# A two-block sequence model on one core: selection pinned on VectorE with new tick prices, and the MLP's two input parts in one matmul

## The chip, the core and the metric

The kernel runs on one core of one Trainium2 chip. Time is device time in microseconds (us) from a run of the whole program; the number that counts is the median of the runs. TensorE (PE) multiplies, VectorE (DVE) and ScalarE (ACT) do the elementwise work, GpSimd (POOL) issues the gathers, SyncE (SP) issues the weight loads.

## The reference

256 tokens of width 2048 pass through two blocks. Only the parts that the change touches are spelled out.

```python
# first block, last part
f = jnp.square(jax.nn.relu(rms_norm(h, norm_mlp_pre[i]) @ mlp_w1[i])) @ mlp_w2[i]   # 2048 -> 8192 -> 2048
h = h + rms_norm(f, norm_mlp_post[i])
...
# second block, last part: 16384 experts, 8 heads, 16 experts for each head and token
q = (x @ wq).reshape(B, S, PEER_HEADS, 2, half)
s = jnp.einsum('bshpd,pkd->bshpk', q, subkeys)          # 2 x 128 scores per head
s1, i1 = lax.top_k(s[..., 0, :], PEER_TOPK)
s2, i2 = lax.top_k(s[..., 1, :], PEER_TOPK)
cand_s = s1[..., :, None] + s2[..., None, :]
top_s, pos = lax.top_k(cand_s, PEER_TOPK)
gate = jax.nn.softmax(top_s, axis=-1)
ue = jnp.take(u_tab, it, axis=0)
ve = jnp.take(v_tab, it, axis=0)
act = jax.nn.gelu(jnp.einsum('td,ted->te', xt, ue), approximate=False)
out = jnp.einsum('te,ted->td', gt * act, ve)
```

## The kernel before, in words

Everything is float32. A weight is split into two parts that TensorE takes at its fast rate, `whi` (the rounded value) and `wlo` (the rest), and so is each input: a tile `x[k]` of 128 x 2 x 256 holds the high part of 256 tokens and, behind it without a gap, the low part. A product needs three terms: `whi` by both parts and `wlo` by the high part.

**Blocks.** The unit of the program is a block of 128 x 2048 weights: `chunk` loads it in two halves (SP), writes `whi` on ScalarE and `wlo` on VectorE, and 16 steps of k multiply it into one PSUM tile. Four half-block buffers of each kind hold two blocks, so VectorE can be at most about one block ahead of the one being multiplied. There are 528 blocks. `chunk` is recorded with high priority, so the scheduler may place its work ahead of what was recorded earlier.

- `mm3` does a step of k as three matmuls of 256 columns.
- `mm2` does it as two: `whi` by both parts at once, into the two halves of a PSUM bank, then `wlo` by the high part into the first half. Somebody has to add the halves later. Before the change only the expert stage uses it, with 224 tokens: 448 and 224 columns.

**MLP.** `mlp_groups` runs four groups, each of 16 blocks of `w_m1` (the square of the ReLU goes to tiles `Bx`) and 16 blocks of `w_m2` (added into `acc`): 128 blocks in all.

**Expert stage.** `route` computes the queries (16 blocks of `w_q`) and selects per head; `route_tail` selects among the pairs and builds the tables of experts. One selection of 16 out of a list (`top16`) is five VectorE instructions; there are 32 lists of 128 and 16 of 80. 32 tokens are then done sparsely: `sparse` gathers 256 rows (128 of u, 128 of v; POOL), and VectorE multiplies each. The other 224 tokens are done densely with all the experts: blocks `w_u` (`peer_u`: ScalarE copies one PSUM half to `pu`, VectorE adds the other, ScalarE applies Gelu) and blocks `w_v` (added into `hT`), in 8 groups of 16 and 16.

**What sets the order.** The selection, the tables and the sparse rows are Python generators. `tick(n)` is called after a block and lets the current generator go on for n units; a `yield w` costs w units, and `yield GAP` stops it till the next tick. The constants are the units per block: `TR` in `route`, `TD` in the tail and the table stage, `TSP` for the sparse rows (u blocks, v blocks). `flush()` in the last expert group runs at once what is left. Within this recorded order the scheduler still moves instructions; `keep_in_program_order` ties one behind the last instruction recorded on its engine.

Of the kernel before, what the change touches and what calls it, by code (L numbers as in the profile page):

```python
# [14 lines left out]
ALU = mybir.AluOpType  # L15
# [19 lines left out]
NF = 2  # L35
# [5 lines left out]
NG = 5  # L41
S0 = 6
UPRE = (3, 5, 8, 8)
TR = 1.5
GU = 4
TD = (1.35, 4.95)
NT = 16
PJ = 4
T8 = 2
# [2 lines left out]
NQ = 128 // SP  # L52
QW = 2048 // NQ
NR = 5
TSP = (1.15, 1.6)
WX = 2
NPRE = 64
PG = NPRE // 8
# [190 lines left out]
class Kern:  # L249
# [161 lines left out]
    def mm2(self, w, x, n, p=None, last=True):  # L411


        nc = self.nc
        first = p is None
        if first:
            p = self.psm.tile([128, 512], F32, name="mm")[:, :2 * n].rearrange("p (c t) -> p c t", c=2)
        m = len(w)
        for k in range(m):
            nc.tensor.matmul(p, w[k][0], x[k][:, :, :n], start=(first and k == 0), stop=False)  # L420
            nc.tensor.matmul(p[:, 0], w[k][1], x[k][:, 0, :n], start=False, stop=(last and k == m - 1))  # L421
        return p

    def blocks(self, srcs, x, first=2):

# [539 lines left out]
    def mlp_groups(self, rm):  # L965
        nc = self.nc
        acc = self.accp.tile([128, 16, 256], F32, name="acc")
        ssq = {}
        for g in range(4):
            hid = []  # L970
            for hb, p in enumerate(self.blocks([self.I["w_m1"][16 * g + i] for i in range(16)], self.xs, 1 if g else NF)):
                if (g, hb) == (0, S0):
                    self.push(self.s5_setup())
                self.tick(TS)
                t = self.T([128, 256], "mr")
                nc.vector.scalar_tensor_tensor(t, p, 0.0, rm(), op0=ALU.max, op1=ALU.mult)
                s = self.T([128, 256], "msq")
                nc.scalar.activation(s, t, AF.Square)
                hid.append(self.split("B", hb, s))
            for nb in range(16):  # L980
                if (g, nb) == (3, 8):
                    self.warm_sqrt()
                p = self.mmps()
                self.mm3(p, self.chunk(self.I["w_m2"][16 * g + nb]), hid)
                if g == 0:
                    nc.vector.tensor_copy(acc[:, nb], p)
                else:
                    nc.vector.tensor_tensor(acc[:, nb], acc[:, nb], p, op=ALU.add)
                if g == 3:
                    self.ssq_add(ssq, acc[:, nb])  # L990
        return acc, ssq
# [471 lines left out]

    def top16(self, v, i, src, s2, w):
        V = self.nc.vector
        V.max(out=v[:, 0:8], in_=src)
        V.max_index(out=i[:, 0:8], in_max=v[:, 0:8], in_values=src)
        yield 2 * w
        V.match_replace(out=s2, in_to_replace=v[:, 0:8], in_values=src, imm_value=-3e38)
        V.max(out=v[:, 8:16], in_=s2)  # L1470
        V.max_index(out=i[:, 8:16], in_max=v[:, 8:16], in_values=s2)
        yield 3 * w
# [63 lines left out]
    def route_head(self, h, sc):  # L1536
        for tb in range(2):
            for half in range(2):
                s2 = self.T([128, 128], "rs2")
                yield from self.top16(self.rv[half][:, tb, h], self.ri[half][:, tb, h], sc[tb][:, half], s2, 0.2)  # L1540

    def route_tail(self):
        nc = self.nc
        V = nc.vector
# [12 lines left out]
        for tb in range(2):  # L1557
            for h in range(8):
                s2 = self.T([128, 80], "rs3")
                yield from self.top16(tv[:, tb, h], ti[:, tb, h], cand[:, tb, h], s2, 0.15)  # L1560
        ex = B([128, 2, 8, 16], "rex")
        V.tensor_tensor(ex, tv, tv[:, :, :, 0:1].to_broadcast([128, 2, 8, 16]), op=ALU.subtract)
        for tb in range(2):
# [322 lines left out]
```

## Time and profile before

| | |
|---|---|
| median of 3 runs | 3260.41 us (3260.27 to 3267.97) |
| profiled execution, its own time | 3260.36 us |
| its span, first to last instruction | 3258.6 us |
| PE / PEld / DVE / ACT / POOL busy | 98 / 93 / 75 / 52 / 19 % |

The profile is of one execution that agrees with the median, so differences can be taken from the span. A PE that is busy 98% need not be at full speed: the number of matmuls that start in a stretch of time tells whether it is.

### The profile page before, as it was taken

To read this page: it belongs to the slowest core of one execution; us is meant where nothing else is said; L and a number is where in the kernel's file an instruction comes from. 1 tells how busy PE (TensorE), PEld (TensorE's weight loads), DVE (VectorE), ACT (ScalarE), POOL (GpSimd) and SP (SyncE) were. 2 spreads that over 40 slices of the span, in tenths; PEclk is the share of its full clock that TensorE was granted. 3 is DMA by queue.
4 is the path that set the end of the run, shared out by engine and by line. 5 is a ranking of instruction groups with operands and counts; after the bars stand their busy time and mean duration, and the time that the engine had idled before them with its cause. 6 is when DMAs were issued, how large, how long until landed. Compare 5 with 4: busy or idle time off the path is not lost.

```text
span 3258.6 us, 59733 instructions
## 1 busy us (share of the span) xinstructions
PE 3178.6 (98%) x23207; PEld 3021.6 (93%) x23207; DVE 2429.8 (75%) x4226; ACT 1695.5 (52%) x2556; POOL 618.4 (19%) x669
## 2 busy tenths in 40 slices
PE   8999989999999999999999989999999999999988
PEld 7888989999999999888899989899999999999987
DVE  5577786575756567898968875775888888888876
ACT  5567555363545445454545445565454454454443
POOL 2001130000000011100003001002334344444432
PEclk9999999999999999999999989999999999999999
DMA  8343546575666555544445457678989989989974
GB/s 272 133 128 118 170 138 209 187 230 193 215 201 197 191 162 182 191 156 160 145 148 175 158 189 229 218 253 280 318 285 326 314 286 313 316 288 315 316 243 150
DMA packets 217645, 708.29 MB, mean 217 GB/s; under 512 B 26944, under 2 KB 53200, under 8 KB 215568
## 3 DMA queue, kind: packets, MB, share of 16 engines
q1 hardware_dynamic: 174208, 579.94, 53.2%
q0 software_dynamic: 31728, 100.98, 9.3%
q10 hardware_dynamic: 11424, 23.55, 2.0%
q8 instruction: 182, 2.98, 0.4%
q14 instruction: 103, 0.84, 0.1%
HBM read 668.16 MB, written 35.15 MB: 216 GB/s over the span
## 4 chain that ended last, share of the span: by engine, by line
PE 44%; DVE 8%; ACT 2%; issue 1%; DMA 0%; DVEq 0%; ACTq 0%; SPq 0%
PE mm L420 21%; PE mm L421 10%; DVE wlo L397 3%; PE mm L407 3%; PE mm L408 3%; PE mm L409 3%; PE sm L1657 1%; PE oT L1220 1%; ACT whi L396 1%; DVE spa L1700 1%; DVE Bx L1782 1%; DVE pa L1774 1%; ACT pa L1670 1%; ACT Bx L1779 1%; DVE pu L1668 1%
## 5 line engine op out<-in xcount | busy, mean ns | idle before, releaser
L396 ACT CAST whi<-raw 128x1024 fp32r<-128x1024 f32 x1056 | 1098.3, 1048 | 1131.3 <-PE mm L408 577.7
L397 DVE TENSOR_TENSOR wlo<-raw,whi 128x1024 fp32r<-128x1024 f32 x1056 | 1292.9, 1231 | 505.2 <-ACT whi L396 499.9
L420 PE MATMUL mm<-Ax,whi 128*128 128x448 f32 x2048 | 654.8, 379 | 0.6 <-ACT whi L396 0.6
L420 PE MATMUL mm<-Bx,whi 128*128 128x448 f32 x2048 | 645.5, 376 | 4.0 <-DVE Bx L1782 3.8
L407 PE MATMUL mm<-Bx,whi 128*128 128x256 f32 x2192 | 625.1, 285 | 0.0
L408 PE MATMUL mm<-Bx,whi 128*128 128x256 f32 x2192 | 621.6, 284 | 0.0
L407 PE MATMUL mm<-Ax,whi 128*128 128x256 f32 x2128 | 607.8, 288 | 13.6 <-ACT Ax L449 5.3
L409 PE MATMUL mm<-Bx,wlo 128*128 128x256 f32 x2192 | 620.9, 283 | 0.0
L408 PE MATMUL mm<-Ax,whi 128*128 128x256 f32 x2128 | 607.4, 286 | 2.0 <-DVE Ax L450 1.6
L409 PE MATMUL mm<-Ax,wlo 128*128 128x256 f32 x2128 | 605.2, 285 | 1.5 <-DVE wlo L397 1.5
L421 PE MATMUL mm<-Ax,wlo 128*128 128x224 f32 x2048 | 544.0, 266 | 14.2 <-DVE wlo L397 14.2
L421 PE MATMUL mm<-Bx,wlo 128*128 128x224 f32 x2048 | 539.9, 264 | 0.0
L407 PEld LDWEIGHTS mm<-Ax,whi 128*128 128x128 f32 x2128 | 409.4, 193 | 24.7 <-issue 6.7
L407 PEld LDWEIGHTS mm<-Bx,whi 128*128 128x128 f32 x2192 | 420.2, 192 | 9.5 <-issue 9.3
L408 PEld LDWEIGHTS mm<-Bx,whi 128*128 128x128 f32 x2192 | 420.5, 192 | 2.3 <-issue 2.2
L409 PEld LDWEIGHTS mm<-Bx,wlo 128*128 128x128 f32 x2192 | 420.3, 192 | 1.1 <-issue 1.0
L420 PEld LDWEIGHTS mm<-Bx,whi 128*128 128x128 f32 x2048 | 384.8, 188 | 35.7 <-DVE Bx L1782 5.9
L420 PEld LDWEIGHTS mm<-Ax,whi 128*128 128x128 f32 x2048 | 388.7, 190 | 31.3 <-ACT whi L396 0.8
L408 PEld LDWEIGHTS mm<-Ax,whi 128*128 128x128 f32 x2128 | 410.8, 193 | 6.5 <-DVE Ax L450 2.5
L409 PEld LDWEIGHTS mm<-Ax,wlo 128*128 128x128 f32 x2128 | 410.8, 193 | 4.8 <-DVE wlo L397 2.0
L421 PEld LDWEIGHTS mm<-Ax,wlo 128*128 128x128 f32 x2048 | 394.8, 193 | 17.5 <-DVE wlo L397 17.4
L421 PEld LDWEIGHTS mm<-Bx,wlo 128*128 128x128 f32 x2048 | 391.3, 191 | 0.2 <-DVE wlo L397 0.2
(465 smaller groups left out, 3256.6 us busy)
## 6 DMA issues: line engine op xcount, KB each, us to landing
raw<-in_w_m SPq DMA_DIRECT2D x256, 512.0 KB, 4.5
raw<-in_w_u SPq DMA_DIRECT2D x256, 512.0 KB, 5.0
raw<-in_w_v SPq DMA_DIRECT2D x256, 512.0 KB, 5.8
raw<-in_w_z SPq DMA_DIRECT2D x156, 512.0 KB, 3.7
raw<-in_w_o SPq DMA_DIRECT2D x64, 512.0 KB, 3.6
raw<-in_w_pg SPq DMA_DIRECT2D x32, 512.0 KB, 4.5
raw<-in_w_q SPq DMA_DIRECT2D x32, 512.0 KB, 3.6
gdr<-gt ACTq DMA_DIRECT2D x14, 1024.0 KB, 4.9
```

The costliest lines, as they stand in the source:

```text
L396: nc.scalar.copy(hi, raw)
L397: nc.vector.tensor_tensor(lo, raw, hi, op=ALU.subtract)
L407: nc.tensor.matmul(p, w[k][0], x[k][:, 0], start=(first and k == 0), stop=False)
L408: nc.tensor.matmul(p, w[k][0], x[k][:, 1], start=False, stop=False)
L409: nc.tensor.matmul(p, w[k][1], x[k][:, 0], start=False, stop=(last and k == n - 1))
L420: nc.tensor.matmul(p, w[k][0], x[k][:, :, :n], start=(first and k == 0), stop=False)
L421: nc.tensor.matmul(p[:, 0], w[k][1], x[k][:, 0, :n], start=False, stop=(last and k == m - 1))
L1220: nc.tensor.matmul(yp[32 * j:32 * j + 32, :256], cw[:, w, j], src, start=(n == 0), stop=(n == 3), tile_position=(0, 32 * j))
L1657: nc.tensor.matmul(p[:, 128 * r:128 * r + 128], A[:, q, :, r], b[:, q, :, r], start=(i == 0), stop=(i == 1))
L1668: nc.vector.tensor_tensor(t, t, p[:, 0], op=ALU.add)
L1670: nc.scalar.activation(a, t, AF.Gelu)
L1700: ins = V.scalar_tensor_tensor(acc, r, w[:, i:i + 1], acc, op0=ALU.mult, op1=ALU.add)
```

## The change

Four things. In `mlp_groups` the blocks are multiplied with `mm2` at 256 tokens (512 and 256 columns) in place of `mm3`, and ScalarE and VectorE add the two PSUM halves; `blocks2` is the new helper for it. In `top16` the first max and the match_replace are tied to the recorded order. The units that a selection costs go up (0.2 to 0.35 and 0.15 to 0.27), and with them the units per block (`TR`, `TD`). The sparse rows get more units per block (`TSP`).

```diff
-TR = 1.5
+TR = 2.6
-TD = (1.35, 4.95)
+TD = (2.0, 4.95)
-TSP = (1.15, 1.6)
+TSP = (1.2, 1.68)
...
+    def blocks2(self, srcs, x, first=2):
+
+        ws = [self.chunk(s) for s in srcs[:first]]
+        ps = [None] * len(ws)
+        for k in range(len(x)):
+            for i, w in enumerate(ws):
+                ps[i] = self.mm2(w[k:k + 1], x[k:k + 1], 256, p=ps[i], last=(k == len(x) - 1))
+        yield from ps
+        for s in srcs[first:]:
+            yield self.mm2(self.chunk(s), x, 256)
...
                 t = self.T([128, 256], "mr")
-                nc.vector.scalar_tensor_tensor(t, p, 0.0, rm(), op0=ALU.max, op1=ALU.mult)
+                nc.scalar.copy(t, p[:, 1])
+                nc.vector.tensor_tensor(t, t, p[:, 0], op=ALU.add)
+                nc.vector.scalar_tensor_tensor(t, t, 0.0, rm(), op0=ALU.max, op1=ALU.mult)
...
-                p = self.mmps()
-                self.mm3(p, self.chunk(self.I["w_m2"][16 * g + nb]), hid)
+                p = self.mm2(self.chunk(self.I["w_m2"][16 * g + nb]), hid, 256)
                 if g == 0:
-                    nc.vector.tensor_copy(acc[:, nb], p)
+                    nc.scalar.copy(acc[:, nb], p[:, 1])
                 else:
-                    nc.vector.tensor_tensor(acc[:, nb], acc[:, nb], p, op=ALU.add)
+                    nc.vector.tensor_tensor(acc[:, nb], acc[:, nb], p[:, 1], op=ALU.add)
+                nc.vector.tensor_tensor(acc[:, nb], acc[:, nb], p[:, 0], op=ALU.add)
...
-        V.max(out=v[:, 0:8], in_=src)
+        self.tc.keep_in_program_order(V.max(out=v[:, 0:8], in_=src))
...
-        V.match_replace(out=s2, in_to_replace=v[:, 0:8], in_values=src, imm_value=-3e38)
+        self.tc.keep_in_program_order(V.match_replace(out=s2, in_to_replace=v[:, 0:8], in_values=src, imm_value=-3e38))
```

In `route_head` and `route_tail` the last argument of `top16` becomes 0.35 and 0.27.

**VectorE, the blocks after the last query block.** Here `route_tail` selects among the 80 pairs of each head (`rcd` holds them, `rtv` and `rti` the winners, `rs` the list with the first eight struck out). Before:

```order
L397 TENSOR_TENSOR wlo<-raw,whi 128x1024
L1668 TENSOR_TENSOR pu<-pu,mm 128x224
L1470 MAX rtv<-rs_22731 128x8
L1467 MAX_INDEX rti<-rtv,rcd 128x8
L1471 MAX_INDEX rti<-rtv,rs_22731 128x8
L1469 MATCH_REPLACE rs_22788<-rtv,rcd 128x80
L1466 MAX rtv<-rcd 128x8
L1470 MAX rtv<-rs_22788 128x8
L1467 MAX_INDEX rti<-rtv,rcd 128x8
L1471 MAX_INDEX rti<-rtv,rs_22788 128x8
L1469 MATCH_REPLACE rs_22794<-rtv,rcd 128x80
L1466 MAX rtv<-rcd 128x8
```

And now:

```order
L397 TENSOR_TENSOR wlo<-raw,whi 128x1024 x2
L1681 TENSOR_TENSOR pu<-pu,mm 128x224
L1482 MATCH_REPLACE rs_21223<-rtv,rcd 128x80
L1483 MAX rtv<-rs_21223 128x8
L1484 MAX_INDEX rti<-rtv,rs_21223 128x8
L1479 MAX rtv<-rcd 128x8
L1480 MAX_INDEX rti<-rtv,rcd 128x8
L1482 MATCH_REPLACE rs_21280<-rtv,rcd 128x80
L1483 MAX rtv<-rs_21280 128x8
L1484 MAX_INDEX rti<-rtv,rs_21280 128x8
L397 TENSOR_TENSOR wlo<-raw,whi 128x1024 x2
L1681 TENSOR_TENSOR pu<-pu,mm 128x224
```

Before, 30 selection instructions stand between this `wlo` and the next and 25 more ahead of the one after it, and the whole tail stands within five blocks. Now seven or eight stand behind the `pu` of each block, over some twenty blocks, and then the tables follow, within three blocks.

**VectorE, the last expert group.** `spa` sums the sparse rows, `pa` and `Bx` belong to the dense u blocks, and the four `hT<-hT,sm` add the sparse result, which TensorE has transposed. Before:

```order
L1668 TENSOR_TENSOR pu<-pu,mm 128x224
L1774 TENSOR_TENSOR pa<-pa,G 128x224
L1782 TENSOR_TENSOR Bx_36137<-pa,Bx_36137 128x224
L1700 SCALAR_TENSOR_TENSOR spa<-row,spw,spa 128x512 x3
L397 TENSOR_TENSOR wlo<-raw,whi 128x1024
L1700 SCALAR_TENSOR_TENSOR spa<-row,spw,spa 128x512 x3
L1722 TENSOR_TENSOR hT<-hT,sm 128x4x32 x4
L397 TENSOR_TENSOR wlo<-raw,whi 128x1024
```

And now:

```order
L1681 TENSOR_TENSOR pu<-pu,mm 128x224
L1787 TENSOR_TENSOR pa<-pa,G 128x224
L1795 TENSOR_TENSOR Bx_33880<-pa,Bx_33880 128x224
L1713 SCALAR_TENSOR_TENSOR spa<-row,spw,spa 128x512
L1795 TENSOR_TENSOR Bx_33884<-st,Bx_33884 128x224
L397 TENSOR_TENSOR wlo<-raw,whi 128x1024
L1735 TENSOR_TENSOR hT<-hT,sm 128x4x32
L397 TENSOR_TENSOR wlo<-raw,whi 128x1024
L1681 TENSOR_TENSOR pu<-pu,mm 128x224
```

Six rows stood together at the start of the group's v blocks, with TensorE's four transposes inside the first v block. Now the last row stands alone seven blocks earlier, and the transposes stand between two u blocks.

**TensorE, inside an MLP block.** Each step of k loads weights before each matmul. Before:

```order
L407 MATMUL mm<-Ax_5396,whi 128x256
L408 MATMUL mm<-Ax_5396,whi 128x256
L409 MATMUL mm<-Ax_5396,wlo 128x256
L407 MATMUL mm<-Ax_5404,whi 128x256
L408 MATMUL mm<-Ax_5404,whi 128x256
```

And now:

```order
L420 MATMUL mm<-Ax_5396,whi 128x512
L421 MATMUL mm<-Ax_5396,wlo 128x256
L420 MATMUL mm<-Ax_5404,whi 128x512
L421 MATMUL mm<-Ax_5404,wlo 128x256
L420 MATMUL mm<-Ax_5412,whi 128x512
```

The columns of a step stay 768; the matmuls, and the weight loads with them, go from three to two.

## Rows read from the trace of the kernel before

**Rows 1.** The page: engines' busy time, share of the span, instructions.

```profile
PE 3178.6 (98%) x23207; PEld 3021.6 (93%) x23207; DVE 2429.8 (75%) x4226; ACT 1695.5 (52%) x2556; POOL 618.4 (19%) x669
```

**Rows 2.** Windows of 80 us: busy, (x instructions); PEclk, DMA share, GB/s end it.

```profile
560.00:640.00 80.00, 80.00 (x669) 80.00 (x669) 39.69 (x42) 29.32 (x28) 0.00 (x0) 1.00 0.57 183
640.00:720.00 80.00, 80.00 (x670) 80.00 (x669) 58.57 (x104) 50.78 (x82) 7.53 (x14) 1.00 0.69 224
...
2320.00:2400.00 80.00, 80.00 (x512) 76.30 (x512) 68.28 (x121) 35.61 (x42) 37.91 (x34) 1.00 0.93 329
```

**Rows 3.** Windows of 10 us around the end of the selection, same columns.

```profile
1870.00:1880.00 10.00, 6.46 (x33) 5.42 (x32) 10.00 (x71) 0.36 (x2) 0.00 (x0) 0.80 0.22 80
1880.00:1890.00 10.00, 9.07 (x30) 8.04 (x31) 9.90 (x39) 5.76 (x8) 0.54 (x1) 0.52 0.35 116
1890.00:1900.00 10.00, 6.04 (x35) 4.97 (x33) 9.76 (x14) 2.52 (x4) 0.54 (x1) 1.00 0.37 116
1900.00:1910.00 10.00, 6.84 (x32) 6.19 (x33) 8.44 (x13) 4.49 (x7) 1.08 (x2) 0.84 0.45 138
...
1920.00:1930.00 10.00, 10.00 (x66) 9.54 (x65) 5.47 (x7) 5.35 (x8) 1.09 (x2) 1.00 0.80 278
```

**Rows 4.** Windows of 10 us in the last expert group, same columns.

```profile
3140.00:3150.00 10.00, 10.00 (x65) 9.54 (x65) 8.51 (x14) 6.09 (x12) 3.99 (x2) 1.00 0.77 248
3150.00:3160.00 10.00, 5.87 (x38) 5.32 (x36) 8.27 (x14) 6.28 (x11) 3.72 (x3) 0.97 0.85 260
3160.00:3170.00 10.00, 5.50 (x21) 5.18 (x22) 3.87 (x8) 0.83 (x1) 0.00 (x0) 0.52 0.29 100
```

**Rows 5.** Timeline of VectorE there: start, duration; idle before and its releaser.

```profile
3157.38 2.32 DVE L1700 SCALAR_TENSOR_TENSOR spa<-row,spw,spa 128x512 f32<-128x512 f32 x3
...
3160.75 1.53 DVE L1700 SCALAR_TENSOR_TENSOR spa<-row,spw,spa 128x512 f32<-128x512 f32 x2
3163.69 0.75 DVE L1700 SCALAR_TENSOR_TENSOR spa<-row,spw,spa 128x512 f32<-128x512 f32 x1 [1.41 <-DMA row<-in_v_rows,osp]
```

**Rows 6.** Timeline of VectorE in a quiet u block.

```profile
1968.85 1.23 DVE L397 TENSOR_TENSOR wlo<-raw,whi 128x1024 fp32r<-128x1024 f32 x1 [0.87 <-ACT whi L396]
1969.99 0.38 DVE L1668 TENSOR_TENSOR pu<-pu,mm 128x224 f32<-128x224 f32 x1
1971.77 1.22 DVE L397 TENSOR_TENSOR wlo<-raw,whi 128x1024 fp32r<-128x1024 f32 x1 [1.40 <-ACT whi L396]
```

**Rows 7.** Timeline of VectorE in the selection's tail and the tables.

```profile
1869.57 0.23 DVE L1470 MAX8 rtv<-rs 128x8 f32<-128x80 f32 x1
...
1870.49 0.22 DVE L1470 MAX8 rtv<-rs 128x8 f32<-128x80 f32 x1
...
1883.16 0.57 DVE L1562 TENSOR_TENSOR rex<-rtv 128x256 f32<-128x256 f32 x1
...
1905.81 0.74 DVE L1606 TENSOR_TENSOR roh<-roh 128x512 f16<-128x512 f16 x2
1906.47 1.22 DVE L397 TENSOR_TENSOR wlo<-raw,whi 128x1024 fp32r<-128x1024 f32 x1
```

**Rows 8.** Timeline of PE in the expert stage: steps of `mm2` at 224 tokens.

```profile
2419.88 0.37 PE L420 MATMUL mm<-Ax,whi 128*128 128x448 f32 x1
2420.09 0.26 PE L421 MATMUL mm<-Ax,wlo 128*128 128x224 f32 x1
2420.19 0.38 PE L420 MATMUL mm<-Ax,whi 128*128 128x448 f32 x1
```

**Rows 9.** Groups by line and shape, 560 to 1200 us: x count | busy, mean ns | idle before.

```profile
L976 DVE SCALAR_TENSOR_TENSOR mr<-mm,rstd 128x256 f32<-128x256 f32 x48 | 20.2, 421 | 16.8 <-PE mm L409 16.8
L988 DVE TENSOR_TENSOR acc<-acc,mm 128x256 f32<-128x256 f32 x48 | 20.2, 421 | 31.9 <-PE mm L409 31.9
```

**Rows 10.** Groups by line, 1700 to 2110 us, ScalarE.

```profile
L1667 ACT COPY pu<-mm 128x224 f32<-128x224 f32 x43 | 14.5, 338 | 0.0
```

More of the change, by code (lines that the diff above doesn't have):

```diff
@@ L970, in mlp_groups @@
             hid = []
-            for hb, p in enumerate(self.blocks([self.I["w_m1"][16 * g + i] for i in range(16)], self.xs, 1 if g else NF)):
+            for hb, p in enumerate(self.blocks2([self.I["w_m1"][16 * g + i] for i in range(16)], self.xs, 1 if g else NF)):
                 if (g, hb) == (0, S0):
@@ L1539, in route_head @@
                 s2 = self.T([128, 128], "rs2")
-                yield from self.top16(self.rv[half][:, tb, h], self.ri[half][:, tb, h], sc[tb][:, half], s2, 0.2)
+                yield from self.top16(self.rv[half][:, tb, h], self.ri[half][:, tb, h], sc[tb][:, half], s2, 0.35)
     def route_tail(self):
@@ L1559, in route_tail @@
                 s2 = self.T([128, 80], "rs3")
-                yield from self.top16(tv[:, tb, h], ti[:, tb, h], cand[:, tb, h], s2, 0.15)
+                yield from self.top16(tv[:, tb, h], ti[:, tb, h], cand[:, tb, h], s2, 0.27)
         ex = B([128, 2, 8, 16], "rex")
```

## The prediction

> **What bounds the kernel now.** I read the page first. TensorE and its weight loads are busy nearly throughout, VectorE three quarters [rows 1]. So two things can shorten the kernel: fewer nanoseconds for the same matmuls, and the removal of stretches where TensorE stands still. Busy time does not tell these apart, so I next read windows and counted matmuls. In the MLP 669 start in 80 us, 119.6 ns each; with `mm2` at 224 tokens 512 start in 80 us, 156.25 ns each, or 312.5 ns for a pair [rows 2]. TensorE is back to back in both stages. I then looked for windows whose count falls below this, and for each of them what VectorE did.
>
> There are two such places in reach of the change. From 1870 to 1910 us, 33 + 30 + 35 + 32 = 130 matmuls start where a quiet stretch has 65.5 in 10 us, 262 in all [rows 3]. The missing 132 are **20.2 us**. VectorE is at 10.0, 9.9, 9.8 and 8.4 of 10 there, and the granted clock falls to 0.52 in one window: between the levels of 1.2 and 2.4 GHz, after TensorE had waited. This is the selection and its tables, standing in VectorE's queue ahead of the `wlo` that TensorE needs. From 3150 to 3170 us 38 + 21 start in place of 130 [rows 4]: **10.8 us**, with the clock at 0.52 once more. There VectorE does six sparse rows in one piece, and TensorE's transposes stand behind them [rows 5].
>
> **The change, part by part.** *Selection.* The selection work is the same; its place is what changes. In a quiet u block VectorE has two idle pieces, 1.40 us behind `pu` and 0.87 us behind the next `wlo`, each until ScalarE delivers `whi` [rows 6]. One selection from 80 takes 0.92 us for its five instructions, start to start [rows 7]; seven or eight of them, as the order now puts behind each `pu`, take 1.3 to 1.5 us. They fill the first idle piece. In the lists of 128 the order puts five to eight behind a `pu`; at a quarter more for each (about 0.24 us, an estimate from the 0.92 and 128 against 80 columns) that is 1.2 to 1.9 us, at most 0.5 us over, and the second idle piece takes it up. The wait that the tie adds costs nothing either: a tied max stands behind a `pu`, which VectorE had to do there anyway, and what queues behind it is a `wlo` whose `whi` ScalarE delivers no sooner.
>
> What is late next: the tables. From `rex` at 1883.16 to the `wlo` at 1906.47 VectorE does, apart from five `wlo` and two `pu`, 23.3 - 5 x 1.13 - 2 x 0.30 = 17.1 us of work (a `wlo` counted by the 1.13 us to the next start) [rows 6, 7]. The order now puts these within five half blocks, together with 0.5 us of selection: 17.6 us where the idle pieces hold 3 x 1.40 + 2 x 0.87 = 5.9 us. VectorE falls 11.7 us behind. Before it reaches TensorE, the lead must go. Four half-block buffers allow about one block, 5.0 us, and in a quiet stretch VectorE waits for ScalarE, so it has that lead. A stall of **6.7 us** remains, bounds 4 (ScalarE delays less than I think) and 12 (no lead). Net: 20.2 - 6.7 = **13.5 us** gained, bounds 8 to 16.
>
> *Sparse rows.* 64 u blocks at 0.05 and about 105 v blocks at 0.08 give 3.2 + 8.4 = 11.6 units more, and two more blocks fall in the gathering stage, as the selection's tail ends two blocks sooner. Six rows were left over. So the last row now comes ahead of the last group's v blocks, as the order shows, and the 10.8 us go. A row costs VectorE 0.75 us [rows 5]; at 0.05 to 0.08 more rows per block this is 0.04 to 0.06 us more per block, where VectorE is busy 8.5 of 10 us [rows 4]. TensorE's transposes now stand between two u blocks, less than a block behind the last row: between nothing and 1.5 us of waiting (two rows). Taken: **10.8 us** gained, and 1 us lost to these two, bounds 0 to 3.
>
> *MLP.* 128 blocks of 16 steps, 2048 steps, each now 3 x 119.6 = 358.8 ns. No row shows 512 columns, so the new step is bounded from the two shapes that there are [rows 2].
> - If time is proportional to columns: 119.6 / 256 = 0.467 and 312.5 / 672 = 0.465 ns per column. Both steps have 768 columns: nothing is gained, 357 to 359 ns. By the start of the next matmul 0.21 us after 448 columns [rows 8], 0.469 ns per column, it could be 360 ns, a loss of 2.5 us in all.
> - If a matmul has a fixed part a and b per column: a + 256 b = 119.6 and 2 a + 672 b = 312.5 give b = 0.458, a = 2.3. The new step is 768 x 0.458 + 4.6 = 356.4 ns: 2.4 ns gained, 4.9 us in all.
> - If the excess over 2.4 columns per ns (12.9 ns for 256 columns, 32.5 ns for the pair) belongs to each piece that lies without a gap in memory, the pair has three pieces of 224, 10.8 ns each, and the new step two, of 512 and 256: 320 + 2 x 10.8 to 2 x 12.9 = 341.6 to 345.8 ns. 13 to 17 ns gained, 27 to 35 us in all.
>
> The first two fit the rows as they are, the third explains why the excess is nearly the same for a piece of 224 and of 256 while the new tile has no gap. I take 6 ns, **12.3 us**, between them; both ends stay for the range.
>
> The row has 119.6 ns for 256 columns [rows 2]. The Trainium skill, page "TensorE: Matmul & The Clock Gate", section "Wait — 56ns, not 53.3ns?", states columns / 2.4 plus about 2.5 ns for a matmul, which is 109.2 ns. The trace does not agree with that. What the rule would make of the dropped matmul is 2.5 ns a step, 5.1 us in place of 12.3, and 3233 us for the kernel.
>
> The price of it: two more instructions for each PSUM tile, a copy on ScalarE (0.34 us at 224 columns) and an addition on VectorE (0.42 us) [rows 9, 10]. VectorE's busiest MLP window goes from 58.6 by 14 blocks x 0.42 to 64.5 of 80 us [rows 2]: no new bound. Four PSUM tiles are in rotation and a block takes 5.6 us, so two engines' 0.8 us don't hold TensorE. Only where `w_m2` starts is somebody waited for: the last `Bx` is needed 45 matmuls, 5.4 us, after its block ends; its chain gets 0.8 us longer, and at the end of the MLP one addition more lies on the path. Cover gone, this would be 0.8 us in each of five places, 4 us. Taken: **0.5 us**.
>
> **The sum.** The profiled execution took 3260.36 us of its own, span 3258.6, and the median is 3260.41: the difference of 0.05 is nothing. 3260.4 - 13.5 - 10.8 - 12.3 + 1.0 + 0.5 = 3225.3, say **3225 us**.
>
> **The rivals.**
> - *The MLP gains by pieces.* For it: the third reading above, 10.8 and 12.9 ns being so close. Against it: 448 columns start the next 0.21 us later and 224 columns 0.10 us [rows 8], just double, as with proportional cost. 31 us in place of 12.3: 3207 us.
> - *The MLP gains nothing.* For it: 0.467 and 0.465. Against it: the two-part input of 448 columns has a gap in memory that the new one has not. 3225 + 12 = 3237 us, and to 3240 if the step is 360 ns.
> - *The stalls move, they don't go.* The tables' work finds no lead (12 us in place of 6.7), and the last rows keep TensorE waiting (10.8 us gained becomes 5): 3225 + 5 + 6 = 3236 us. For it: all of the tables' work is still in one piece. Against it: VectorE is idle 45% of a quiet block [rows 3].
> - *The tie makes each u block longer; the other side.* If VectorE's work per u block were one after the other with ScalarE's, that is, if the selection stood ahead of `pu` (on which the Gelu and the next `whi` on ScalarE wait), 1.4 to 1.9 us would be added to each of some 24 blocks: about 40 us, which gives 3265 us. It decides from 1.4 us a block. For it: in four of ten microseconds VectorE waits for ScalarE, so the two work as a ring [rows 3, 6]. Against it: the order now has the selection behind `pu`.
>
> **How the numbers follow.** Forecast (MLP 5 to 20 us, selection and rows as reckoned; 3216 to 3234) 0.50; by pieces (3200 to 3215) 0.21; nothing (3234 to 3242) 0.18; stalls move (3232 to 3245) 0.06; longer blocks 0.05. The range leaves out the last case and the outer parts of the others: 3204 to 3243 us. The forecast's own is 3216 to 3234. A measurement of this kernel can tell 0.3%, 10 us, from no change: faster below 3250.6. The first four cases are all there: 0.94 faster with a part of the last one left to the others; 0.03 same, 0.03 slower.
>
> **What would show it.** In the changed kernel's windows: MLP counts of 2 x 80 / (0.3528) = 453 matmuls in 80 us for 6 ns; 446 for nothing, 463 to 468 by pieces. No window of the u blocks under 60 in 10 us, but where the tables stand, with about 7 us lost in all. No window under 60 in the last expert group. `wlo` in the u blocks released by ScalarE, as before. The prediction is wrong if 512 columns take other than 233 to 237 ns, if the u blocks count fewer than 64 in 10 us throughout, or if the tables cost 12 us or more.

## The result and the profile after

| | before | after |
|---|---|---|
| median of 6 runs each | 3261.57 us (3256.85 to 3267.97) | 3227.11 us (3219.66 to 3230.87) |
| ratio, 95% interval | | 0.9891 [0.988, 0.9902] |
| profiled execution, own time and span | 3260.36 / 3258.6 us | 3220.75 / 3219.0 us |

The change makes the kernel 1.1% faster; 3225 us was forecast. Runs of one kernel lie up to 11 us apart, so what a part of the change is worth is read from the traces, not from single times.

The page of the kernel after, to be held against [rows 1]:

```profile
PE 3156.0 (98%) x21159; PEld 2905.9 (90%) x21159; DVE 2477.2 (77%) x4338; ACT 1719.9 (53%) x2636; POOL 611.3 (19%) x669
```

There are 2048 matmuls fewer, one for each step of the MLP. TensorE is busy 98% as before, so the page doesn't tell where the time came from. Windows of the kernel after do. First the MLP, the 512-column matmuls (line 420) alone, one for each step; the columns are TensorE's busy time and count, the granted clock, the DMA share and GB/s:

```profile
480.00:560.00 80.00, 79.83 (x226) 1.00 0.63 218
...
1040.00:1120.00 80.00, 79.92 (x231) 1.00 0.57 198
```

The eight windows from 480 to 1120 us hold 226 to 231 steps each, 1824 in all: 350.9 ns a step. Of the kernel before, the trace holds 1778 first matmuls of a step in the same stretch, 360.0 ns each. So 9.1 ns a step, and 2048 x 9.1 = **18.6 us**.

Next the windows of all engines that answer to [rows 3] and [rows 4], in the kernel after: the selection (1890 to 1900), the tables (the middle one of three windows from 1960 to 1990), the last group of experts (3150 to 3160).

```profile
1890.00:1900.00 10.00, 10.00 (x66) 9.54 (x65) 9.62 (x30) 5.12 (x9) 1.64 (x3) 1.00 0.58 202
...
1970.00:1980.00 10.00, 7.12 (x29) 6.38 (x28) 9.76 (x13) 2.74 (x5) 0.54 (x1) 0.66 0.34 115
...
3150.00:3160.00 10.00, 10.00 (x65) 9.54 (x65) 6.42 (x9) 4.86 (x6) 2.73 (x3) 1.00 0.65 214
```

The selection now costs TensorE nothing: 65 to 67 matmuls in every window from 1850 to 1960, at VectorE's 8 to 9.6 of 10. The tables take 64 + 29 + 64 = 157 where 196.5 would stand: 6.0 us lost by this count. A window's count also takes in matmuls that began before it, so the starts are more exact. In the kernel after, 64 steps of `mm2` at the tables stand between these two:

```profile
1959.91 0.37 PE L420 MATMUL mm<-Ax,whi 128*128 128x448 f32 x1
...
1986.64 0.38 PE L420 MATMUL mm<-Ax,whi 128*128 128x448 f32 x1
```

They take 26.73 us. The same 64 steps of the kernel before, which has its tables behind it by then, take 20.05 (1997.70 to 2017.75 us). So the tables cost **6.7 us**, against 20.1 by the starts for selection and tables before (20.2 by the windows). The pause of 10.8 us in the last group is gone.

VectorE's timeline in the kernel after, at the selection and at the first steps of the tables:

```profile
1931.06 1.23 DVE L397 TENSOR_TENSOR wlo<-raw,whi 128x1024 fp32r<-128x1024 f32 x1 [0.20 <-ACT whi L396]
1932.20 0.38 DVE L1681 TENSOR_TENSOR pu<-pu,mm 128x224 f32<-128x224 f32 x1
1932.50 0.24 DVE L1479 MAX8 rtv<-rcd 128x8 f32<-128x80 f32 x1
...
1934.32 1.20 DVE L397 TENSOR_TENSOR wlo<-raw,whi 128x1024 fp32r<-128x1024 f32 x1
...
1969.87 1.23 DVE L1612 TENSOR_TENSOR roh<-rio,rij 128x2048 f16<-128x2048 f16 x1
...
1972.28 1.22 DVE L397 TENSOR_TENSOR wlo<-raw,whi 128x1024 fp32r<-128x1024 f32 x1
```

Between `pu` and the next `wlo` the selection fills 1932.50 to 1934.32, the piece that was idle [rows 6], and the `wlo` ahead still ends a wait for ScalarE. At the tables the `wlo` at 1972.28 comes behind 4 us of table work, and TensorE's timeline in the kernel after shows what that does:

```profile
1970.29 0.38 PE L420 MATMUL mm<-Ax,whi 128*128 128x448 f32 x1
1973.55 0.56 PE L421 MATMUL mm<-Ax,wlo 128*128 128x224 f32 x1 [2.88 <-DVE wlo L397]
1973.90 0.60 PE L420 MATMUL mm<-Ax,whi 128*128 128x448 f32 x1
...
1974.49 0.60 PE L420 MATMUL mm<-Ax,whi 128*128 128x448 f32 x1
```

TensorE waits 2.88 us, and behind the wait pairs start 0.59 us apart in place of 0.31, at a granted clock of 0.66 in that window (1.2 GHz for a part of it, 2.4 for the rest). No other wait of TensorE's matmuls is listed from 1959 to 1990 us. So the wait is under half of the 6.7 us, and most of the rest is the lower clock after it.

All waits of TensorE for VectorE from 1700 to 3200 us in the kernel after (operation, what it waited for; us in total, times, longest):

```profile
PE mm L421 <- DVE wlo L397: 7.5, 7, 2.9
PE mm L420 <- DVE Bx L1795: 4.7, 6, 1.8
```

The kernel before has 14.2 us for `wlo` in nine places there, 3.8 for `Bx` in six, and 8.6 us in one for the rows' sum `spa`, which is no longer in the list.

### The profile page after: what moved, and what is told of

Read it like the earlier page. It is cut to its first block, busy times and chain, and to the rows that moved or that the text cites. A ratio compares the mean times of both kernels' runs of the same rounds, so it can differ in the third digit from the quotient of the medians.

```text
span 3219.0 us, 55735 instructions
## 1 busy us (share of the span) xinstructions
PE 3156.0 (98%) x21159; PEld 2905.9 (90%) x21159; DVE 2477.2 (77%) x4338; ACT 1719.9 (53%) x2636; POOL 611.3 (19%) x669
## 4 chain that ended last, share of the span: by engine, by line
PE 43%; DVE 7%; ACT 3%; issue 1%; DMA 1%; POOL 0%; SPq 0%; DVEq 0%; ACTq 0%; POOLq 0%
PE mm L420 20%; PE mm L421 10%; PE mm L407 3%; PE mm L408 3%; PE mm L409 3%; DVE wlo L397 3%; PE sm L1670 1%; ACT whi L396 1%; PE oT L1233 1%; DVE Bx L1795 1%; DVE pa L1787 1%; ACT pa L1683 1%; ACT Bx L1792 1%; DVE spa L1713 1%; DVE pu L1681 1%
## 5 line engine op out<-in xcount | busy, mean ns | idle before, releaser
L420 PE MATMUL mm<-Ax,whi 128*128 128x448 f32 (+1 forms) x3072 | 1017.6, 386 | 8.0 <-DVE Ax L461 7.2
L420 PE MATMUL mm<-Bx,whi 128*128 128x448 f32 (+1 forms) x3072 | 1004.2, 383 | 4.8 <-DVE Bx L1795 4.7
L421 PE MATMUL mm<-Ax,wlo 128*128 128x224 f32 (+1 forms) x3072 | 831.2, 271 | 9.1 <-DVE wlo L397 8.9
L421 PE MATMUL mm<-Bx,wlo 128*128 128x224 f32 (+1 forms) x3072 | 824.9, 269 | 0.0
L420 PEld LDWEIGHTS mm<-Ax,whi 128*128 128x128 f32 x3072 | 581.9, 189 | 86.2 <-DVE Ax L461 8.7
L420 PEld LDWEIGHTS mm<-Bx,whi 128*128 128x128 f32 x3072 | 576.0, 187 | 84.0 <-DVE Bx L1795 6.7
L407 PE MATMUL mm<-Bx,whi 128*128 128x256 f32 x1168 | 335.3, 287 | 0.0
L408 PE MATMUL mm<-Bx,whi 128*128 128x256 f32 x1168 | 331.8, 284 | 0.0
L409 PE MATMUL mm<-Bx,wlo 128*128 128x256 f32 x1168 | 331.1, 284 | 0.0
L407 PE MATMUL mm<-Ax,whi 128*128 128x256 f32 x1104 | 317.8, 289 | 6.0 <-ACT Ax L457 5.2
L408 PE MATMUL mm<-Ax,whi 128*128 128x256 f32 x1104 | 316.3, 287 | 0.1
L409 PE MATMUL mm<-Ax,wlo 128*128 128x256 f32 x1104 | 314.8, 286 | 0.9 <-DVE wlo L397 0.9
L407 PEld LDWEIGHTS mm<-Bx,whi 128*128 128x128 f32 x1168 | 223.7, 192 | 9.5 <-issue 9.3
L407 PEld LDWEIGHTS mm<-Ax,whi 128*128 128x128 f32 x1104 | 212.7, 193 | 15.6 <-issue 5.7
L408 PEld LDWEIGHTS mm<-Bx,whi 128*128 128x128 f32 x1168 | 224.0, 192 | 2.3 <-issue 2.2
```

The lines of the kernel that those rows point to most:

```text
L407: nc.tensor.matmul(p, w[k][0], x[k][:, 0], start=(first and k == 0), stop=False)
L408: nc.tensor.matmul(p, w[k][0], x[k][:, 1], start=False, stop=False)
L409: nc.tensor.matmul(p, w[k][1], x[k][:, 0], start=False, stop=(last and k == n - 1))
```

## The experiments

Four kernels make one part of the change alone on the kernel before. Each is a single run, and the kernel before took 3263.15 us beside them.

**The MLP alone.**

```diff
-                self.mm3(p, self.chunk(self.I["w_m2"][16 * g + nb]), hid)
+                p = self.mm2(self.chunk(self.I["w_m2"][16 * g + nb]), hid, 256)
```

Likewise `w_m1` with `blocks2`, and the copies and additions of the two halves, as in the change.

> The kernel before with the MLP part of the change alone (a 512-column and a 256-column matmul in place of three of 256). If the whole of what the MLP of the changed kernel gained (453 to 465 matmuls per 80 us where 446 stood) is its own, this run shows the same rates, 14 to 22 us off the span (about 3236 to 3245), and the expert stage as in the kernel before: 130 of 262 matmuls in 1870 to 1910 shifted by the gain, the pause of the last group of experts still there. Rival: part of the MLP's gain came from the other edits; then the rates stay at 446 to 451 and the gain is under 10 us.

Measured: 3241.20 us, 22 less. Line 420 alone, in a window of this kernel:

```profile
560.00:640.00 80.00, 80.00 (x232) 1.00 0.57 191
```

From 480 to 1120 us there are 1832 steps, 349.3 ns each, 10.7 less than before: 21.9 us, or 20.8 by the starts of the first and the last step of the MLP (more of it than in the kernel after stands at the quicker of two paces, of which below). The burst of the selection and the pause at the end are still there (26 + 41 + 28 matmuls from 1860 to 1890, 49 + 19 from 3130 to 3150). The gain of the MLP is its own.

**The pins alone.**

```diff
-        V.max(out=v[:, 0:8], in_=src)
+        self.tc.keep_in_program_order(V.max(out=v[:, 0:8], in_=src))
...
-        V.match_replace(out=s2, ...)
+        self.tc.keep_in_program_order(V.match_replace(out=s2, ...))
```

> The kernel before with only the two pins of the selection (the first maximum and the replacing step stay where the program has them), the old weights of time kept. Theory: what ends the burst behind the last expert block of the first half is the pins, because an instruction that isn't pinned is put later by the scheduler; then the 20 us of the selection and tables fall to 3 to 10, the span is about 3245 to 3252, and the selection stands in the idle pieces of the u blocks. Rival: the pins alone do nothing, since the old weights hand the steps out too late to stand behind the blocks; then the 130 of 262 matmuls of the burst are still there and the span is 3256 to 3261.

**The weights of time alone.**

```diff
-TR = 1.5
+TR = 2.6
-TD = (1.35, 4.95)
+TD = (2.0, 4.95)
```

With them 0.2 becomes 0.35 and 0.15 becomes 0.27, as in the change.

> The kernel before with only the new weights of time (1.5 to 2.6, 1.35 to 2.0, .2 to .35 and .15 to .27), no pins. Theory that the pins do it: the weights alone leave the same number of steps beside each block and the scheduler still defers them, the burst stays, span 3256 to 3262. Rival, that the weights do it: the steps come earlier in the program, the burst is gone or under 8 us, span 3244 to 3252.

Measured: pins 3250.16 us, 13.0 less; weights 3269.26 us, 6.1 more. TensorE's windows of the kernel with the pins, where the tables stand:

```profile
1970.00:1980.00 10.00, 7.47 (x46) 1.00 0.38 116
1980.00:1990.00 10.00, 6.73 (x40) 1.00 0.40 120
```

A window of all engines in the kernel with the weights, the last of four from 1880 to 1920 us:

```profile
1910.00:1920.00 10.00, 5.70 (x30) 5.17 (x31) 8.92 (x14) 3.36 (x6) 0.70 (x2) 0.93 0.39 118
```

With the pins the burst is gone (65 or 66 in each window from 1870 to 1920), and 131 - 86 = 45 matmuls are missing at the tables, 6.9 us. With the weights the burst stands as it was: 41 + 32 + 32 + 30 = 135 of 262 matmuls in the four windows, 19.4 us. The pins do it, the weights don't. That this run is longer isn't their doing: the u blocks behind the queries begin at 1864.8 us, in the profiled kernel before at 1853.7, and those 11 us are lost ahead of 1664 us, in stages that the edit doesn't touch. The stages that the weights touch take as long as before or 1 us less, by the starts of their first and last matmuls.

**The rows per block alone.**

```diff
-TSP = (1.15, 1.6)
+TSP = (1.2, 1.68)
```

> The kernel before with only the rows gathered per block raised (1.15 to 1.2 and 1.6 to 1.68). Theory: the six rows and their transposes that stood behind the last w_v block of the last group now fit in ahead; the pause of 10.8 us goes, the span falls by 9 to 11 to about 3248, everything else stays. Rival: they only fit in because the selection and tables end earlier in the changed kernel; then rows are still left over at the end, and the gain is under 5 us.

Measured: 3257.07 us, 6.1 less. One of TensorE's windows of this kernel, and its wait for `wlo` from 2260 to 2350 us, around the first of the eight expert groups, whose v blocks begin at 2309 us:

```profile
3150.00:3160.00 10.00, 10.00 (x65) 1.00 0.60 199
```

```profile
PE mm L421 <- DVE wlo L397: 2.6, 3, 1.3
```

The pause is gone with the selection as late as ever. There are 65 or more matmuls in every window from 3130 to 3190 us. So the raised rows are enough by themselves, and the rival falls. The price is in the second fence: three waits, 2.6 us, where the kernel before has none for `wlo`, and the kernel after has 1.2 us. The rest of what is short of the 10.8 us lies in stretches that the edit doesn't touch (from 1320 to 1360 us, for one, the granted clock is 0.92 and 0.82, where the kernel before has 1.00).

**The change without its weights.** A single run; the kernel before took 3260.09 us beside it.

```diff
-TR = 2.6
+TR = 1.5
-TD = (2.0, 4.95)
+TD = (1.35, 4.95)
```

0.35 and 0.27 go back to 0.2 and 0.15.

> The changed kernel with the old weights of time (2.6 back to 1.5, 2.0 to 1.35, .35 to .2 and .27 to .15); the pins, the rows and the MLP of the change stay. Theory: the weights give nothing, they only move about 5 us of stall from the selection to the tables and the table stage's transposes ahead; then blocks 256 to 352 take the same time within 3 us, and the last group of experts has no pause, since the raised rows alone bring that. Profiled time 3217 to 3226. Rival: without the weights the tail ends later and rows are left for the end again, or the selection runs late: 3230 or more.

Measured: 3221.05 us, span 3219.3 against 3219.0 of the kernel after. The tables, in this kernel's windows:

```profile
1950.00:1960.00 10.00, 6.83 (x35) 0.87 0.39 135
1960.00:1970.00 10.00, 8.70 (x53) 0.96 0.47 158
```

131 - 88 = 43 matmuls are missing, 6.6 us, and the last group has 65 or 66 in every window. The weights of time are worth nothing that these runs can tell.

**The token tile without its gap.** This kernel and the next two were run four times each; the kernel before took 3261.26 us beside them, the median of seven.

```diff
+    def xtile2(self, st, k):
+        x = self.xtile(st, k).rearrange("p c t -> p (c t)")
+        return x[:, :2 * ND2].rearrange("p (c t) -> p c t", c=2)
...
-                    x = self.xtile("A", k)
+                    x = self.xtile2("A", k)
```

> The changed kernel with the two parts of a token tile of the expert stage side by side, 224 + 224 columns without the gap of 32 that now lies between them; nothing else. In the expert stage a matmul of 448 columns holds 211 to 215 ns until the next and one of 224 100 to 102 (313 a pair, .466 ns a column); in the MLP, where the parts lie without a gap, 512 hold 233 and 256 117 (350 a pair, .455 to .457 a column). Theory that a matmul over a gap pays for two pieces: the pair falls to 303 to 308 ns, 4096 pairs give 20 to 40 us, time 3187 to 3207. Rival, that a matmul costs a fixed part and a part per column wherever its columns lie: the pair stays at 313 and the time at 3220 to 3230.

Measured: 3222.77 us, 0.9891 [0.9874, 0.9908], no different from the change. TensorE's timeline of this kernel in the expert stage:

```profile
2350.03 0.38 PE L420 MATMUL mm<-Bx,whi 128*128 128x448 f32 x1
2350.24 0.27 PE L421 MATMUL mm<-Bx,wlo 128*128 128x224 f32 x1
2350.35 0.37 PE L420 MATMUL mm<-Bx,whi 128*128 128x448 f32 x1
```

0.21 and 0.11 us, with the gap 0.21 and 0.10 [rows 8]. The gap costs nothing; that theory falls.

**The tables held in order.**

```diff
-        V.tensor_copy(pf, tif)
+        self.tc.keep_in_program_order(V.tensor_copy(pf, tif))
...
-                V.tensor_tensor(oh, oh, ix[i][:, tb].unsqueeze(2).to_broadcast([128, 16, 16, 8]), op=ALU.mult)
+                self.tc.keep_in_program_order(V.tensor_tensor(oh, oh, ix[i][:, tb].unsqueeze(2).to_broadcast([128, 16, 16, 8]), op=ALU.mult))
```

Likewise `ex`, the max of `fi`, both `ij` and the `is_equal` of `oh`, and in `build_g` the `is_equal` of `A` and `B0`.

> The changed kernel with nine operations of the tables and three of the first gate building held to the program's order on VectorE. Theory: the 6 to 7 us that TensorE loses at the tables (blocks 296 to 300) come from a burst of table steps set ahead of the w_v splits by the scheduler; held in place they lie in the idle pieces of the blocks behind, 4 to 6 us less, and up to 5 more at the first gate building: 3216 to 3222. Rival: held steps only make VectorE's queue longer in order, the splits wait as before or later ones do: no gain within 2 us, or a loss of up to 5.

Measured: **3212.43 us** (3208.93 to 3216.14), 0.9856 [0.9839, 0.9872]. This is faster than the change: the intervals don't touch, and the run with the tile without gap, 3222.77, was made on the same chip. VectorE's timeline of this kernel at the tables:

```profile
1969.61 0.38 DVE L1681 TENSOR_TENSOR pu<-pu,mm 128x224 f32<-128x224 f32 x1
1969.91 0.75 DVE L1602 TENSOR_SCALAR rij<-rfi 128x256 f16<-128x256 f32 x1
1970.70 1.23 DVE L1612 TENSOR_TENSOR roh<-rio,rij 128x2048 f16<-128x2048 f16 x1
1971.84 2.35 DVE L397 TENSOR_TENSOR wlo<-raw,whi 128x1024 fp32r<-128x1024 f32 x2
```

And its windows there:

```profile
1970.00:1980.00 10.00, 10.00 (x66) 9.54 (x65) 8.53 (x10) 6.46 (x11) 1.62 (x3) 1.00 0.85 268
1980.00:1990.00 10.00, 9.83 (x64) 9.16 (x63) 9.76 (x15) 3.62 (x6) 0.54 (x1) 1.00 0.56 197
```

The table steps now stand behind a `pu` and are broken by a `wlo` in time. TensorE loses next to nothing, and the clock stays at 1.00. The waits of TensorE for `wlo` from 1950 to 2060 us, 4.8 us in two places in the kernel after, are gone. By the starts, the 64 steps that took 26.73 us take 20.05 again, 6.7 less, and the u blocks behind them, with the first gate building, take 5.0 less. So both gains that the theory named are there. The median lies below the 3216 to 3222 expected; the profiled executions differ by 11.9 us (3219.0 against 3207.1 of span), the medians by 14.7.

**Both of these.** Its edit is the two diffs above.

> The changed kernel with both of the edits: the token tiles of the expert stage without a gap, and the tables' and the first gate building's operations held to the program's order. If both help and a shorter u block leaves VectorE enough room, the gains add up: 3180 to 3200. Rival: a pair of 303 ns makes each u block 2 us shorter, the splits and selection then set the time in the u blocks, and the sum is 5 to 15 us short of the two gains.

Measured: 3214.10 us, 0.9857 [0.984, 0.9874]: the tables' gain and nothing for the tile, as each had shown.

The next three ask what a matmul costs in the MLP. Each is a single run, with the kernel before at 3260.09 us.

**The MLP with the sizes of the expert stage.**

```diff
+            if n == 256 and not (first and k == 0):
+                nc.tensor.matmul(pf[:, :448], w[k][0], xf[:, :448], start=False, stop=False)
+                nc.tensor.matmul(pf[:, :224], w[k][1], xf[:, :224], start=False, stop=(last and k == m - 1))
+                continue
```

> The changed kernel with the MLP's matmuls cut from 512 and 256 columns to 448 and 224, the sizes of the expert stage, in all but the first step of a block; 48 of 512 columns and 32 of 256 are left out. Theory that a matmul has a fixed part of about 15 ns and .417 ns a column: a pair, now 350 ns, takes 310 to 313 as in the expert stage, the MLP 2048 pairs by 37 to 40, so 70 to 77 us less. Rival, that time goes with the columns (.456 ns each) and the expert stage has a price of its own: 306 ns, 84 us less.

**Half of the second matmul.**

```diff
-            nc.tensor.matmul(p[:, 0], w[k][1], x[k][:, 0, :n], ...)
+            nl = 128 if n == 256 else n
+            nc.tensor.matmul(p[:, 0, :nl], w[k][1], x[k][:, 0, :nl], ...)
```

> The changed kernel with the MLP's second matmul on 128 of its 256 columns; the low part of the weights is left out for the other half of the tokens. Theory of a fixed part of about 15 ns and .417 ns a column: a pair falls from 350 to 297 ns, 2048 of them by 109 us. Proportional: to 292 ns, by 119 us. Rival that a matmul can't be shorter than the load of its weights, which is what the three of 120 ns in the kernel before were held by: the second stays at 100 to 117 ns, the pair at 333 to 350, and no more than 35 us are gained.

**A second matmul of 512 columns.**

```diff
+            if n == 256:
+                nc.tensor.matmul(p, w[k][1], x[k], start=False, stop=(last and k == m - 1))
```

> The changed kernel with the MLP's second matmul on 512 columns, both parts of the tokens, in place of 256: a product more than the change computes. Theory of a fixed part of about 15 ns and .417 ns a column: a pair rises from 350 to 457 ns, the MLP by 219 us to about 3440. Proportional: to 467 ns, by 239 us, about 3460. If the loads of the weights count, a pair of two equally long matmuls hides both, and it falls under 457.

Measured: 3255.24, 3259.38 and 3429.88 us. The first two do less work than the change and are some 30 us *slower*. Matmuls far apart in undisturbed stretches give the pace: in each fence the first and the last start, with their count behind it. The kernel after, 48 pairs in either piece:

```profile
580.15 0.40 PE L420 MATMUL mm<-Bx,whi 128*128 128x512 f32 x1
...
597.12 0.40 PE L420 MATMUL mm<-Bx,whi 128*128 128x512 f32 x1
...
646.06 0.39 PE L420 MATMUL mm<-Ax,whi 128*128 128x512 f32 x1
...
662.70 0.39 PE L420 MATMUL mm<-Ax,whi 128*128 128x512 f32 x1
```

The kernel with half of the second matmul, 48 pairs:

```profile
580.20 0.44 PE L420 MATMUL mm<-Bx,whi 128*128 128x512 f32 x1
580.48 0.22 PE L422 MATMUL mm<-Bx,wlo 128*128 128x128 f32 x1
...
596.52 0.44 PE L420 MATMUL mm<-Bx,whi 128*128 128x512 f32 x1
```

The kernel with 512 and 512, 64 matmuls:

```profile
580.15 0.39 PE L420 MATMUL mm<-Bx,whi 128*128 128x512 f32 x1
...
594.66 0.39 PE L420 MATMUL mm<-Bx,whi 128*128 128x512 f32 x1
```

So 512 and 256 columns take 353.5 ns in one stretch and 346.7 in another, 512 and 128 take 340.0, 512 and 512 take 453.4. Three of 256 took 360.0, and 448 and 224 in the expert stage 312.5 by the count of [rows 2]. By the starts the 312.5 is 313.3 (64 pairs in 20.05 us). All but the 353.5 fit one rule for the sum of a step, worked out from these rows: a matmul counts columns / 2.4 plus 13.3 ns, and not less than 113.3 ns. 512 gives 226.7, 256 gives 120.0, 448 gives 200.0, and 224 and 128 come to the least. That gives 346.7, 340.0, 453.3, 360.0 and 313.3. The theory of 15 ns and .417 ns a column was near for 512 and 256 columns and low for smaller ones; the proportional one is out (it had 467 and 292).

The single starts don't divide a step in this way. Behind 512 columns the 128 start 0.28 us later (580.20 to 580.48), and the next 512 then follow in 0.06; behind 448 columns the 224 start in 0.21 us and the next in 0.10 [rows 8]. What is alike in these two steps is the weight loads, in the kernel with half of the second matmul:

```profile
580.14 0.19 PEld L420 LDWEIGHTS mm<-Bx,whi 128*128 128x128 f32 x1
580.25 0.19 PEld L422 LDWEIGHTS mm<-Bx,wlo 128*128 128x128 f32 x1
```

Across the short matmul two loads start 0.11 us apart, as they do across the 224 columns (2419.78 and 2419.89 us in the kernel before). This bears out the rival, that the least is the time of a weight load; no run changes the loads alone.

Why less work was slower: a window of all engines in the kernel with 448 and 224 columns, and TensorE's waits in it from 470 to 1140 us.

```profile
880.00:960.00 80.00, 62.44 (x354) 55.65 (x355) 52.78 (x96) 48.55 (x85) 5.38 (x10) 0.93 0.55 194
```

```profile
PE mm L426 <- DVE wlo L397: 30.3, 21, 4.3
PE mm L422 <- DVE Bx L463: 20.4, 5, 8.3
```

TensorE now waits over 50 us for VectorE, at a lower clock in this window, though VectorE is busy only 53 of 80. In the kernel after no wait for `wlo` or `Bx` is listed from 470 to 1200 us. But the edit changed more than the matmuls: with other sizes the scheduler put VectorE's MLP work into another order. The same place in the kernel after, and then in the kernel with 448 and 224 columns, with TensorE's wait behind it:

```profile
904.10 1.22 DVE L397 TENSOR_TENSOR wlo<-raw,whi 128x1024 fp32r<-128x1024 f32 x1
...
907.11 1.22 DVE L397 TENSOR_TENSOR wlo<-raw,whi 128x1024 fp32r<-128x1024 f32 x1
```

```profile
904.92 1.22 DVE L397 TENSOR_TENSOR wlo<-raw,whi 128x1024 fp32r<-128x1024 f32 x1
...
909.52 1.21 DVE L397 TENSOR_TENSOR wlo<-raw,whi 128x1024 fp32r<-128x1024 f32 x1
910.79 0.39 PE L426 MATMUL mm<-Ax,wlo 128*128 128x256 f32 x1 [0.87 <-DVE wlo L397]
```

Between the two `wlo` stand four instructions in the first and nine in the second. The longest work between two `wlo` of the MLP is 2.5 us in the kernel after, 4.7 with 448 and 224 columns, and 3.4 with half of the second matmul. The kernel with 512 and 512 has nearly the order of the latter, also with 3.4 us, and no wait is listed in it from 470 to 1300 us, at 453.4 ns a step. So the order doesn't stop TensorE at a slow pace; whether the order of the kernel after would keep up with 313 or 340 ns a step, no run shows. The slowdown came with both, a new order and a quicker pace; whether either would do it alone stays open.

**Two steps at a time in the MLP**, on the version with the tables held in order.

```diff
+        if n == 256 and m == 16:
+            for k in range(0, m, 2):
+                nc.tensor.matmul(p, w[k][0], x[k][:, :, :n], start=(first and k == 0), stop=False)
+                nc.tensor.matmul(p, w[k + 1][0], x[k + 1][:, :, :n], start=False, stop=False)
+                nc.tensor.matmul(p[:, 0], w[k][1], x[k][:, 0, :n], start=False, stop=False)
+                nc.tensor.matmul(p[:, 0], w[k + 1][1], x[k + 1][:, 0, :n], start=False, stop=(last and k == m - 2))
```

> The changed kernel with the tables' operations held in order (the version that measured 3212 us), and in the MLP's undivided blocks the two matmuls of 512 columns of two steps ahead of their two of 256, in place of one and one. In the changed kernel a pair stands at 347 ns in some stretches and at 354 in others, for whole blocks on end, and changes between the two at block bounds. Theory that the alternation of long and short matmuls lets it settle in either, and that two of a kind next to each other have one pace: 694 ns for four in all stretches, the eight half groups at 89.0 us each where four to six of them stand at 90.5, 5 to 9 us less: about 3205. Rival, that a matmul's price depends on its neighbour (a weight load hides behind a long one and not behind two short ones in a row): the four take over 700 ns, up to 20 us more.

Measured: **3208.91 us** (3203.01 to 3209.66), 0.9832 [0.9815, 0.9848], with the kernel before at 3263.58 us. 24 fours in this kernel, by its rows at 580.42 and 597.14:

```profile
580.42 0.40 PE L421 MATMUL mm<-Bx,whi 128*128 128x512 f32 x1
...
597.14 0.40 PE L421 MATMUL mm<-Bx,whi 128*128 128x512 f32 x1
```

They take 696.7 ns each, 348.3 a step, and the stretches of 353 are gone. This is the theory's direction: by the starts of the first and the last step the MLP takes 728.5 us, against 732.3 in the version with the tables held in order and 733.6 in the kernel after; the 694 ns were not reached. The interval reaches into that of the tables' version, so that the 3.5 us between them is the order's is likely and not shown by times. It is the fastest kernel of the study.

## Why the prediction was right, step by step

- *What bounds the kernel.* TensorE back to back, with the two places that lose time. One is gone and the other smaller. This mechanism held, and so did the stalls' sizes; one term, the MLP, was half again as large as reckoned.
- *Selection, 13.5 us.* Measured 20.1 - 6.7 = 13.4. The steps behind `pu` in the idle pieces cost nothing (65 to 67 matmuls in each window), as reckoned, and the `wlo` is still released by ScalarE. The runs with pins and weights apart show what the forecast had left together: the pins alone make the gain, the weights none.
- *Tables, a stall of 6.7 us.* Measured 6.7, but the working behind it isn't what happened. It had all of the 6.7 us as waiting. TensorE waited 2.88 us, so more was covered than thought, and the lower clock after the wait, which the working had at nothing, took about as much again. Two errors of opposite sign: that the sum is right is luck.
- *Rows per block, 10.8 us.* Gone in full, and by the rows alone; the two blocks that I let the selection's earlier end add were not needed. *Its price, 1.0 us* (0 to 3): 2.3 by the starts. The u blocks between the tables and the first v block take 1.8 us more than before, and from there to the last matmul it is 10.3 us less where 10.8 were to go. The rows alone show the same: 2.2 and 1.0. At the first group the `wlo` waits are 1.2 us where there were none, and over all groups those for `Bx` rise from 3.8 to 4.7 us.
- *MLP, 12.3 us.* The mis-sized term: 18.6 measured, 9.1 ns a step in place of 6. Of the 3.1 ns, 1.2 are a reading: the windows' count gave 119.6 ns for 256 columns, a step of three is 360.0 ns in place of 358.8. The rest is the new step, 350.9 in place of 352.8. The gain lies between the readings "fixed part" (2.4 ns) and "by pieces" (13 to 17), and neither was right. By the rule above there is a fixed part, but of 13.3 ns for each matmul. The pair of 224 tokens, from which I worked out 2.3, hides it, because its smaller matmul already stands at the least of 113.3. The rule of the Trainium skill, page "TensorE: Matmul & The Clock Gate", section "Wait — 56ns, not 53.3ns?", has 2.5 ns in its place; the trace doesn't agree for these matmuls, and the measured 13.3 decides. By pieces would need the gap to cost something, which the tile without gap excludes. The sign that I had named, 233 to 237 ns for 512 columns, tells nothing here: by the starts the next matmul follows 512 columns in 230 to 241 ns in the kernel after, 236 in the mean from 560 to 660 us, which is about that range whatever the rule; the step as a whole decides. For the least of 113.3 ns the same page of the Trainium skill, section "LDWEIGHTS (loading the stationary operand)", has a price that is near: a load takes the columns of the weights / 1.2 in ns, an estimate of 106.7 ns for 128. The loads 0.11 us apart agree with that.
- *MLP price, 0.5 us.* The copy takes 364 ns and the addition 413, near the 0.34 and 0.42 reckoned; the kernel after, by line, from 470 to 1200 us:

```profile
L988 DVE TENSOR_TENSOR mr<-mr,mm 128x256 f32<-128x256 f32 x64 | 26.4, 413 | 0.0
L987 ACT COPY mr<-mm 128x256 f32<-128x256 f32 x64 | 23.3, 364 | 0.0
```

  At the starts of `w_m2` no wait of TensorE's matmuls is listed, and its weight loads wait for `Bx` 0.6 us in two places from 560 to 1120 us. VectorE's busiest window is 66.3 of 80, where 64.5 was expected.
- *The sum.* By the starts the MLP takes 733.6 us in place of 752.5, and -13.4 - 10.8 - 18.9 + 2.3 = -40.8, where the span fell by 39.6. The stages ahead of the MLP, which the change doesn't touch, took 1.3 us longer in the profiled execution (the MLP's first step is at 444.1 us, before at 442.8), and that is the difference. The forecast had 35.1 us, and the medians fell by 34.5. That they agree so well is in part luck: the two profiled executions, from which the parts are read, differ by 39.6, and the MLP alone gave 6.6 more than its term.
- *The rivals.* MLP by pieces and MLP nothing are excluded by the 350.9 ns. Stalls that move: the tables' 6.7 us are what is left of that. A longer u block: no window of the selection is under 65.

## What to carry to other kernels

A scheduler that may put work later can pile it up ahead of the next thing that everybody waits for, as it did here; holding a few instructions of each step behind an operation that has to stand there anyway spread it, and weights of time didn't replace that. Where two shapes are to tell a fixed cost from one per column, look first whether the smaller one stands at a least time, since a fit through it gives a fixed part that is far too small. An edit to one engine can make the scheduler reorder another: here smaller matmuls came with another order on VectorE, and a kernel that does less work was slower. So compare the orders before laying such a result to the pace alone.

## What was not expected of the hardware

- After a wait of 2.88 us TensorE's pairs started 0.59 us apart in place of 0.31, at a granted clock of 0.66 in that window, and the tables cost 6.7 us in all, more than twice the wait.
- The same pair of 512 and 256 columns stands at 346.7 or at 353.5 ns for whole blocks, with nobody waiting and the granted clock at 1.00. With two long and two short matmuls in turn it takes 348.3 throughout. What decides between the two paces stays open.
- 128 columns in place of 256 behind 512 make the step only 6.7 ns shorter (340.0 in place of 346.7), and across the short matmul the weight loads start 0.11 us apart.
